# Batched 64x64 matrix products: two output rows to a partition, and all DMAs on one queue

## The chip, the cores and the metric

One core of a Trainium2 chip. The metric is the device time in microseconds of one execution, slowest core (there is only one). Engines are named as in the profile: PE (TensorE), PEld (its weight loads), DVE (VectorE), ACT (ScalarE), POOL (GpSimd), SP (SyncE). DMAs are issued from an engine's queue and carried by 16 DMA engines. DMAs issued from POOL use what the profile calls queue 0, "software_dynamic"; those issued from SP use queue 1, "hardware_dynamic".

## The reference

```python
# a, b: [1024, 64, 64] float32, normally distributed
def reference(a, b):
    return np.matmul(a, b).astype(np.float32)
```

16.8 MB of each input are read and 16.8 MB are written. A row of a matrix is 64 floats, 256 contiguous bytes.

## The kernel before

The batch is worked in 16 groups of 64 matrices. Loads are issued from POOL and cast fp32 to bf16 on the way. PE transposes `a`, multiplies, DVE and ACT copy the products out of PSUM, and SP issues the stores.

```python
    a_v = a.rearrange("(g u hc) r n -> g hc r u n", u=U_LG, hc=4)
    b_v = b.rearrange("(g s h) r n -> g h r s n", s=S_LG, h=2)
    o_v = out.rearrange("(g s h) r n -> g h r s n", s=S_LG, h=2)
    ...
    for lg in range(n_lg):
        a_ld = lg_pool.tile([128, U_LG, 128], bf16, name="a_ld")
        b_ld = lg_pool.tile([128, S_LG, 64], bf16, name="b_ld")
        # loads: nc.gpsimd.dma_start(...), 4 for a and 2 for b, runs of 256 bytes in DRAM
        ...
        o_sb = lg_pool.tile([128, S_LG, 64], fp32, name="o_sb")
        for cg in range(n_cg):
            # 8 transposes of 128x128, one copy to at_sb, 32 products of 64x64, copies to o_sb
            ...
        for s0 in range(0, S_LG, S_CG):
            nc.sync.dma_start(
                out=o_v[lg, :, :, s0 : s0 + S_CG, :],
                in_=o_sb[:, s0 : s0 + S_CG, :],
            )
```

In `o_v` a partition is one row of a matrix, so each contiguous piece of a store is one row: 256 bytes.

Of the kernel before, what the change touches and what calls it, by code (L numbers as in the profile page):

```python
# [1 line left out]

# [5 lines left out]

fp32 = mybir.dt.float32  # L10
bf16 = mybir.dt.bfloat16


@with_exitstack
def kernel(
    ctx: ExitStack,
    tc: tile.TileContext,
    a: bass.AP,
    b: bass.AP,
    out: bass.AP,  # L20
):
    nc = tc.nc

    B, M, K = a.shape
    _, _, N = b.shape
    assert (M, K, N) == (64, 64, 64)

    LG = 64 if B % 64 == 0 else 32
    CG = 32
    CAST_ON_DMA = True  # L30
    SBUF_BUFS = 3
    PSUM_BUFS = 2

    assert B % LG == 0 and LG % CG == 0
    n_lg = B // LG
    n_cg = LG // CG

    U_LG = LG // 4
    S_LG = LG // 2
    U_CG = CG // 4  # L40
    S_CG = CG // 2
    BANK_SLOTS = 8

    a_v = a.rearrange("(g u hc) r n -> g hc r u n", u=U_LG, hc=4)
    b_v = b.rearrange("(g s h) r n -> g h r s n", s=S_LG, h=2)
    o_v = out.rearrange("(g s h) r n -> g h r s n", s=S_LG, h=2)

    consts = ctx.enter_context(tc.tile_pool(name="consts", bufs=1))
    lg_pool = ctx.enter_context(tc.tile_pool(name="lg", bufs=SBUF_BUFS))
    cg_pool = ctx.enter_context(tc.tile_pool(name="cg", bufs=2 * PSUM_BUFS))  # L50
    ps_pool = ctx.enter_context(
        tc.tile_pool(name="ps", bufs=PSUM_BUFS, space=bass.MemoryType.PSUM)
    )

    identity = consts.tile([128, 128], bf16)
    make_identity(nc, identity)

    for lg in range(n_lg):
        ld_dt = bf16 if CAST_ON_DMA else fp32
        a_ld = lg_pool.tile([128, U_LG, 128], ld_dt, name="a_ld")  # L60
        b_ld = lg_pool.tile([128, S_LG, 64], ld_dt, name="b_ld")

        for h in range(2):
            for c in range(2):
                nc.gpsimd.dma_start(  # L65
                    out=a_ld[64 * h : 64 * h + 64, :, 64 * c : 64 * c + 64],
                    in_=a_v[lg, 2 * h + c],
                )
        for s0 in range(0, S_LG, S_CG):
            nc.gpsimd.dma_start(  # L70
                out=b_ld[:, s0 : s0 + S_CG, :],
                in_=b_v[lg, :, :, s0 : s0 + S_CG, :],
            )

        if CAST_ON_DMA:
            a_sb, b_sb = a_ld, b_ld
        else:
            a_sb = lg_pool.tile([128, U_LG, 128], bf16, name="a_sb")
            b_sb = lg_pool.tile([128, S_LG, 64], bf16, name="b_sb")
            nc.vector.tensor_copy(a_sb[:], a_ld[:])  # L80
            nc.scalar.copy(b_sb[:], b_ld[:])

        o_sb = lg_pool.tile([128, S_LG, 64], fp32, name="o_sb")

        for cg in range(n_cg):
            u0 = cg * U_CG
            s_base = cg * S_CG

            at_ps = ps_pool.tile([128, U_CG, 128], bf16, name="at_ps")
            for uu in range(U_CG):  # L90
                nc.tensor.transpose(  # L91
                    at_ps[:, uu, :], a_sb[:, u0 + uu, :], identity
                )
            at_sb = cg_pool.tile([128, U_CG, 128], bf16, name="at_sb")
            nc.vector.tensor_copy(at_sb[:], at_ps[:])  # L95

            o_ps = ps_pool.tile([128, S_CG, 64], fp32, name="o_ps")
            for sl in range(S_CG):
                s = s_base + sl
                for h in range(2):  # L100
                    rows = slice(64 * h, 64 * h + 64)
                    nc.tensor.matmul(  # L102
                        o_ps[rows, sl, :],
                        at_sb[rows, sl // 2, 64 * (sl % 2) : 64 * (sl % 2) + 64],
                        b_sb[rows, s, :],
                        start=True,
                        stop=True,
                    )

            for k in range(0, S_CG, BANK_SLOTS):  # L110
                src = o_ps[:, k : k + BANK_SLOTS, :]
                dst = o_sb[:, s_base + k : s_base + k + BANK_SLOTS, :]
                if (cg + k // BANK_SLOTS) % 2 == 0:
                    nc.vector.tensor_copy(dst, src)  # L114
                else:
                    nc.scalar.copy(dst, src)  # L116

        for s0 in range(0, S_LG, S_CG):
            nc.sync.dma_start(
                out=o_v[lg, :, :, s0 : s0 + S_CG, :],  # L120
                in_=o_sb[:, s0 : s0 + S_CG, :],
            )


# [1 line left out]
_INS = ['a', 'b']  # L126
_OUTS = [((1024, 64, 64), 'float32')]


# [23 lines left out]
```

## Time and profile before

| | before |
|---|---|
| median of 5 runs | 222.24 us (221.48 to 223.13) |
| span in the profile | 220.5 us |
| busy: PE, DVE, ACT | 29%, 20%, 9% |
| DMA packets: loads, stores | 131,072, 65,536 |

These are lines from the page of the kernel before. The first gives busy time and share of the span by engine. `DMA` and `GB/s` are 40 slices of the span: tenths of the DMA engines' time, and what they moved. The `q` lines give packets, MB and the packets' summed time as a share of 16 engines' span (packets overlap, so it can pass 100%). Then come the chain of waits by engine ("issue" is time in which an engine waited for nothing that the profile shows), and the DMA issues with the size of one and its time to landing.

```profile
span 220.5 us, 3019 instructions
PE 63.7 (29%) x1280; PEld 56.7 (26%) x1280; DVE 44.3 (20%) x64; ACT 20.0 (9%) x33; POOL 89.8 (41%) x102
...
DMA  7999999999999999999999999999999999999974
GB/s 49 139 155 158 159 158 158 158 158 156 158 158 159 158 156 161 157 158 158 157 158 158 158 157 158 158 160 158 157 157 159 155 158 157 158 159 156 169 149 95
...
q0 software_dynamic: 132608, 16.78, 117.7%
q1 hardware_dynamic: 66048, 16.78, 55.7%
...
DMA 81%; POOL 13%; issue 3%; PE 0%; DVE 0%; ACT 0%; POOLq 0%
...
out_dram<-o_sb SPq DMA_DIRECT2D x32, 512.0 KB, 11.0
a_ld<-in_a_dram POOLq DMA_DIRECT2D x64, 128.0 KB, 15.2
b_ld<-in_b_dram POOLq DMA_DIRECT2D x32, 256.0 KB, 20.0
```

DMA stands at 9 from the second slice to nearly the end, it is 81% of the chain, and no compute engine is above 30%. GB/s is a flat 158. A 9 alone does not show that the engines never idle: the digit adds up the packets' times, which overlap (by the q lines, 173% of the span here), and stops at 9. The q lines also count packets of 4 bytes; without them there are 131,072 loads and 65,536 stores.

To see what a packet costs, I counted the trace's packet records in stretches of 4 us and fitted (least squares, leaving out the start and the end) how much of one DMA engine's time each kind takes. Three stretches of the kernel before, and the fit:

```
stretch from the first packet, us   loads   stores   ns of one engine per packet
128 to 132                           4779        0   13.4
152 to 156                           1642     1653   19.4
164 to 168                           1614     1629   19.7
fit: 13.3 ns per load, 25.7 ns per store
sum: 131,072 x 13.3 / 16 = 109 us;  65,536 x 25.7 / 16 = 105 us
```

The two prices together give back the 16 engines' time in every stretch closely (scatter 0.6%), so the engines were busy throughout. "Fit" below always means this.

### The profile page before, as it was taken

To read this page: it belongs to the slowest core of one execution; us is meant where nothing else is said; L and a number is where in the kernel's file an instruction comes from. 1 tells how busy PE (TensorE), PEld (TensorE's weight loads), DVE (VectorE), ACT (ScalarE), POOL (GpSimd) and SP (SyncE) were. 2 spreads that over 40 slices of the span, in tenths; PEclk is the share of its full clock that TensorE was granted. 3 is DMA by queue.
4 is the path that set the end of the run, shared out by engine and by line. 5 is a ranking of instruction groups with operands and counts; after the bars stand their busy time and mean duration, and the time that the engine had idled before them with its cause. 6 is when DMAs were issued, how large, how long until landed. Compare 5 with 4: busy or idle time off the path is not lost.

```text
span 220.5 us, 3019 instructions
## 1 busy us (share of the span) xinstructions
PE 63.7 (29%) x1280; PEld 56.7 (26%) x1280; DVE 44.3 (20%) x64; ACT 20.0 (9%) x33; POOL 89.8 (41%) x102
## 2 busy tenths in 40 slices
PE   0443131142321425123341133403323241222420
PEld 0433121142320414122231133303322231222310
DVE  0223121122211312103131031312113131031211
ACT  2021101102011020200211002110110202001020
POOL 8994441625425354161632427334262542600000
DMA  7999999999999999999999999999999999999974
GB/s 49 139 155 158 159 158 158 158 158 156 158 158 159 158 156 161 157 158 158 157 158 158 158 157 158 158 160 158 157 157 159 155 158 157 158 159 156 169 149 95
DMA packets 198669, 33.74 MB, mean 153 GB/s; under 512 B 198657, under 2 KB 198657, under 8 KB 198657
## 3 DMA queue, kind: packets, MB, share of 16 engines
q0 software_dynamic: 132608, 16.78, 117.7%
q1 hardware_dynamic: 66048, 16.78, 55.7%
q8 instruction: 10, 0.16, 0.3%
q14 instruction: 3, 0.02, 0.0%
HBM read 33.55 MB, written 16.78 MB: 228 GB/s over the span
## 4 chain that ended last, share of the span: by engine, by line
DMA 81%; POOL 13%; issue 3%; PE 0%; DVE 0%; ACT 0%; POOLq 0%
DMA b_ld<-in_b_dram 60%; DMA a_ld<-in_a_dram 21%; POOL a_ld L65 8%; POOL b_ld L70 5%; PE o_ps L102 0%; DVE o_sb L114 0%; ACT o_sb L116 0%; POOL identity masks.py:199 0%; POOL identity masks.py:197 0%; POOLq masks.py:199 0%; POOLq L70 0%; POOLq L148 0%; POOLq L137 0%
## 5 line engine op out<-in xcount | busy, mean ns | idle before, releaser
L65 POOL DMA_DIRECT2D a_ld<-in_a_dram x64 | 52.6, 833 | 86.8 <-DMA b_ld<-in_b_dram 74.9
L102 PE MATMUL o_ps<-b_ld,at_sb 64*64 64x64 bf16 x1024 | 34.0, 238 | 79.0 <-DMA b_ld<-in_b_dram 79.0
L102 PEld LDWEIGHTS <-at_sb 64*64 64x64 bf16 x1024 | 30.6, 151 | 84.3 <-issue 79.1
L91 PE MATMUL at_ps<-identity,a_ld 128*128 128x128 bf16 x256 | 29.8, 309 | 71.6 <-DMA a_ld<-in_a_dram 71.6
L91 PEld LDWEIGHTS <-a_ld 128*128 128x128 bf16 x256 | 26.0, 143 | 73.1 <-issue 68.2
L70 POOL DMA_DIRECT2D b_ld<-in_b_dram x32 | 37.1, 1169 | 15.9 <-DMA a_ld<-in_a_dram 14.3
L114 DVE COPY o_sb<-o_ps 128x512 f32<-128x512 f32 x32 | 22.1, 692 | 100.6 <-ACT o_sb L116 60.7
L116 ACT COPY o_sb<-o_ps 128x512 f32<-128x512 f32 x32 | 18.8, 586 | 194.1 <-DVE o_sb L114 153.8
L95 DVE COPY at_sb<-at_ps 128x1024 bf16<-128x1024 bf16 x32 | 22.1, 692 | 70.8 <-PE at_ps L91 70.8
L116 ACT ACT_TABLE_LOAD x1 | 1.3, 1283 | 0.7 <-PEq L137 0.7
masks.py:199 POOL TENSOR_SCALAR_AFFINE_SELECT identity<-identity 128x128 bf16<-128x128 bf16 x1 | 0.3, 306 | 0.1
masks.py:197 POOL MEMSET identity<- 128x128 bf16 x1 | 0.2, 205 | 0.3 <-POOLq L137 0.3
L137 POOL MEMSET const-float32-0.0<- 128x1 f32 x1 | 0.1, 99 | 0.2 <-issue 0.2
L137 POOL MEMSET const-bfloat16-1.0<- 128x1 bf16 x1 | 0.1, 102 | 0.0
L137 POOL MEMSET const-uint8-127<- 128x1 uint8 x1 | 0.1, 102 | 0.0
L137 POOL MEMSET const-float32-1.0<- 128x1 f32 x1 | 0.1, 99 | 0.0
## 6 DMA issues: line engine op xcount, KB each, us to landing
out_dram<-o_sb SPq DMA_DIRECT2D x32, 512.0 KB, 11.0
a_ld<-in_a_dram POOLq DMA_DIRECT2D x64, 128.0 KB, 15.2
b_ld<-in_b_dram POOLq DMA_DIRECT2D x32, 256.0 KB, 20.0
```

The source lines that it names most:

```text
L65: nc.gpsimd.dma_start(out=a_ld[64 * h : 64 * h + 64, :, 64 * c : 64 * c + 64], in_=a_v[lg, 2 * h + c],)
L70: nc.gpsimd.dma_start(out=b_ld[:, s0 : s0 + S_CG, :], in_=b_v[lg, :, :, s0 : s0 + S_CG, :],)
L91: nc.tensor.transpose(at_ps[:, uu, :], a_sb[:, u0 + uu, :], identity)
L95: nc.vector.tensor_copy(at_sb[:], at_ps[:])
L102: nc.tensor.matmul(o_ps[rows, sl, :], at_sb[rows, sl // 2, 64 * (sl % 2) : 64 * (sl % 2) + 64], b_sb[rows, s, :], start=True, stop=True,)
L114: nc.vector.tensor_copy(dst, src)
L116: nc.scalar.copy(dst, src)
L137: nc = _bacc.Bacc("TRN2", target_bir_lowering=False, num_devices=1)
```

## The change

Three things at once. Stores get runs of 512 contiguous bytes: a partition holds two neighbouring output rows. The stores move from SP's queue to POOL's, behind the loads. The order on POOL is fixed by hand, with loads two groups ahead of the compute. To produce row pairs, `a` is loaded block-diagonally (two matrices on the diagonal of a 128x128 block, zeros kept from one memset), which doubles the transposes, and the products take every second row of `a` as their weights. Smaller things change with it: compute groups of 16 matrices instead of 32, three PSUM buffers instead of two, one store of 1 MB per group (two for the last group) instead of two of 512 KB. The diff's core:

```diff
-    o_v = out.rearrange("(g s h) r n -> g h r s n", s=S_LG, h=2)
+    a_tiles = []
+    for ai in range(A_BUFS):                       # A_BUFS = 3
+        a_diag = a_pool.tile([128, P2_LG, 128], bf16, name=f"a_diag_{ai}")
+        nc.vector.memset(a_diag, 0.0)
+        a_tiles.append(a_diag)
+    def load_a(lg):
+        a_sb = a_tiles[lg % A_BUFS]
+        for h in range(2):
+            nc.gpsimd.dma_start(
+                out=a_sb[64 * h : 64 * h + 64, :, 64 * h : 64 * h + 64],
+                in_=a_v[lg, h],
+            )
     ...
+        o_dst = out[i0 : i0 + LG].rearrange(
+            "(q b4) (t u) c -> b4 t q u c", b4=4, u=2
+        )
     ...
+                for j in range(2):
                     nc.tensor.matmul(
-                        o_ps[rows, sl, :],
-                        at_sb[rows, sl // 2, 64 * (sl % 2) : 64 * (sl % 2) + 64],
-                        b_sb[rows, s, :],
+                        o_ps[orows, sigma, 64 * j : 64 * j + 64],
+                        stat[:, :, j::2],
+                        b_sb[:, p, :],
     ...
-            nc.sync.dma_start(
-                out=o_v[lg, :, :, s0 : s0 + S_CG, :],
-                in_=o_sb[:, s0 : s0 + S_CG, :],
-            )
+                nc.gpsimd.dma_start(out=o_dst[:, :, q0:q1], in_=o_sb[:, q0:q1, :])
+    with tc.manual_schedule(engines={mybir.EngineType.Pool}):
+        load_b(0); load_a(0); load_a(1); load_b(1)      # four lines in the kernel
+        for lg in range(n_lg):
+            if lg + 2 < n_lg:
+                load_a(lg + 2)
+                load_b(lg + 2)
+            compute_and_store(lg)
```

More of the change, by code (lines that the diff above doesn't have):

```diff
@@ L26 @@
     assert (M, K, N) == (64, 64, 64)
-    LG = 64 if B % 64 == 0 else 32
-    CG = 32
-    CAST_ON_DMA = True
+    LG = 64 if B % 64 == 0 else B
+    CG = 16
+    STORE_BF16 = False
+    A_BUFS = 3
     SBUF_BUFS = 3
-    PSUM_BUFS = 2
+    PSUM_BUFS = 3
     assert B % LG == 0 and LG % CG == 0
@@ L36 @@
     n_cg = LG // CG
-    U_LG = LG // 4
-    S_LG = LG // 2
-    U_CG = CG // 4
-    S_CG = CG // 2
-    BANK_SLOTS = 8
-    a_v = a.rearrange("(g u hc) r n -> g hc r u n", u=U_LG, hc=4)
-    b_v = b.rearrange("(g s h) r n -> g h r s n", s=S_LG, h=2)
-    o_v = out.rearrange("(g s h) r n -> g h r s n", s=S_LG, h=2)
+    P2_LG = LG // 2
+    P2_CG = CG // 2
+    S4_CG = CG // 4
+    a_v = a.rearrange("(g p h) r n -> g h r p n", p=P2_LG, h=2)
+    b_v = b.rearrange("(g s h) r n -> g h r s n", s=P2_LG, h=2)
     consts = ctx.enter_context(tc.tile_pool(name="consts", bufs=1))
+    a_pool = ctx.enter_context(tc.tile_pool(name="a_pool", bufs=1))
     lg_pool = ctx.enter_context(tc.tile_pool(name="lg", bufs=SBUF_BUFS))
@@ L56 @@
     make_identity(nc, identity)
-    for lg in range(n_lg):
-        ld_dt = bf16 if CAST_ON_DMA else fp32
-        a_ld = lg_pool.tile([128, U_LG, 128], ld_dt, name="a_ld")
-        b_ld = lg_pool.tile([128, S_LG, 64], ld_dt, name="b_ld")
-        for h in range(2):
-            for c in range(2):
-                nc.gpsimd.dma_start(
-                    out=a_ld[64 * h : 64 * h + 64, :, 64 * c : 64 * c + 64],
-                    in_=a_v[lg, 2 * h + c],
-                )
-        for s0 in range(0, S_LG, S_CG):
-            nc.gpsimd.dma_start(
-                out=b_ld[:, s0 : s0 + S_CG, :],
-                in_=b_v[lg, :, :, s0 : s0 + S_CG, :],
-            )
-        if CAST_ON_DMA:
-            a_sb, b_sb = a_ld, b_ld
-        else:
-            a_sb = lg_pool.tile([128, U_LG, 128], bf16, name="a_sb")
-            b_sb = lg_pool.tile([128, S_LG, 64], bf16, name="b_sb")
-            nc.vector.tensor_copy(a_sb[:], a_ld[:])
-            nc.scalar.copy(b_sb[:], b_ld[:])
-        o_sb = lg_pool.tile([128, S_LG, 64], fp32, name="o_sb")
-        for cg in range(n_cg):
-            u0 = cg * U_CG
-            s_base = cg * S_CG
-            at_ps = ps_pool.tile([128, U_CG, 128], bf16, name="at_ps")
-            for uu in range(U_CG):
-                nc.tensor.transpose(
-                    at_ps[:, uu, :], a_sb[:, u0 + uu, :], identity
-                )
-            at_sb = cg_pool.tile([128, U_CG, 128], bf16, name="at_sb")
-            nc.vector.tensor_copy(at_sb[:], at_ps[:])
-            o_ps = ps_pool.tile([128, S_CG, 64], fp32, name="o_ps")
-            for sl in range(S_CG):
-                s = s_base + sl
-                for h in range(2):
-                    rows = slice(64 * h, 64 * h + 64)
@@ new lines, with load_b @@
+    a_tiles = []
[3 more added lines that the diff above has]
+        a_tiles.append(a_diag)
+    out_dt = bf16 if STORE_BF16 else fp32
+    b_tiles = {}
+    def load_a(lg):
+        a_sb = a_tiles[lg % A_BUFS]
+        for h in range(2):
+            nc.gpsimd.dma_start(
+                out=a_sb[64 * h : 64 * h + 64, :, 64 * h : 64 * h + 64],
+                in_=a_v[lg, h],
+            )
+    def load_b(lg):
+        b_sb = lg_pool.tile([128, P2_LG, 64], bf16, name="b_sb")
+        for s0 in range(0, P2_LG, P2_LG // 2):
+            nc.gpsimd.dma_start(
+                out=b_sb[:, s0 : s0 + P2_LG // 2, :],
+                in_=b_v[lg, :, :, s0 : s0 + P2_LG // 2, :],
+            )
+        b_tiles[lg] = b_sb
@@ new lines, in compute_and_store @@
+    def compute_and_store(lg):
+        i0 = lg * LG
+        a_sb = a_tiles[lg % A_BUFS]
+        b_sb = b_tiles.pop(lg)
+        o_sb = lg_pool.tile([128, LG // 4, 128], out_dt, name="o_sb")
+        o_dst = out[i0 : i0 + LG].rearrange(
+            "(q b4) (t u) c -> b4 t q u c", b4=4, u=2
+        )
+        for cg in range(n_cg):
+            p0 = cg * P2_CG
+            t_ps = ps_pool.tile([128, P2_CG, 128], bf16, name="t_ps")
+            for pp in range(P2_CG):
+                nc.tensor.transpose(
+                    t_ps[:, pp, :], a_sb[:, p0 + pp, :], identity
+                )
+            t_sb = cg_pool.tile([128, P2_CG, 128], bf16, name="t_sb")
+            nc.vector.tensor_copy(t_sb[:], t_ps[:])
+            o_ps = ps_pool.tile([128, S4_CG, 128], fp32, name="o_ps")
+            for pp in range(P2_CG):
+                p = p0 + pp
+                sigma, colp = pp // 2, pp % 2
+                orows = slice(64 * colp, 64 * colp + 64)
+                stat = t_sb[:, pp, :].rearrange("k (hh mm) -> k hh mm", hh=2)
+                for j in range(2):
@@ L108 @@
                     )
-            for k in range(0, S_CG, BANK_SLOTS):
-                src = o_ps[:, k : k + BANK_SLOTS, :]
-                dst = o_sb[:, s_base + k : s_base + k + BANK_SLOTS, :]
-                if (cg + k // BANK_SLOTS) % 2 == 0:
-                    nc.vector.tensor_copy(dst, src)
-                else:
-                    nc.scalar.copy(dst, src)
-        for s0 in range(0, S_LG, S_CG):
-            nc.sync.dma_start(
-                out=o_v[lg, :, :, s0 : s0 + S_CG, :],
-                in_=o_sb[:, s0 : s0 + S_CG, :],
-            )
+            half = S4_CG // 2
+            dst = o_sb[:, cg * S4_CG : (cg + 1) * S4_CG, :]
+            nc.vector.tensor_copy(dst[:, :half, :], o_ps[:, :half, :])
+            nc.scalar.copy(dst[:, half:, :], o_ps[:, half:, :])
+            pieces = 2 if lg == n_lg - 1 else 1
+            if (cg + 1) % (n_cg // pieces) == 0:
+                q1 = (cg + 1) * S4_CG
+                q0 = q1 - (n_cg // pieces) * S4_CG
+                nc.gpsimd.dma_start(out=o_dst[:, :, q0:q1], in_=o_sb[:, q0:q1, :])
+    with tc.manual_schedule(engines={mybir.EngineType.Pool}):
+        load_b(0)
+        load_a(0)
+        load_a(1)
+        load_b(1)
+        for lg in range(n_lg):
[3 more added lines that the diff above has]
+            compute_and_store(lg)
 _INS = ['a', 'b']
```

## The prediction

> **What bounds the kernel now.** DMA. The page's slices show DMA at 9 tenths in nearly every slice and 155 to 160 GB/s, the chain of waits is 81% DMA (60% b loads, 21% a loads), while PE is busy 29%, DVE 20%, ACT 9%. The DMA section counts 131,072 load packets (queue 0; 256 bytes read, 128 written as bf16) and 65,536 store packets of 256 bytes (queue 1).
>
> I counted the trace's packet records in stretches of 4 us. Where only loads run, one engine of the 16 takes 13.3 ns per packet; where loads and stores alternate one to one, 19.4 ns. A least-squares fit gives 13.3 ns per load and 25.7 ns per store. The sum: 131,072 x 13.3 / 16 = 109 us, and 65,536 x 25.7 / 16 = 105 us, together 214 of the 220.5 us span. The other 6.7 us are the start (first packet near 3 us), the fill and the end. So half the time is the stores, at twice the price of a load with the same 256 bytes at the HBM end.
>
> **What the change does.** It pairs two output rows in one partition, so a store moves 512 contiguous bytes: 32,768 store packets instead of 65,536. Loads keep their packets (131,072 of 256 bytes). To get there it doubles the transposes (512 of 128x128, half of each zeros) and keeps 1,024 products of 64 output columns, now over 128 rows.
>
> The price of a 512-byte store is the one disputed term. The Trainium skill's page "DMA: Bandwidth & Descriptors" says in "Specifications" that under 512 bytes the DMA does a read-modify-write, which fits the 25.7 against 13.3 ns here; and in "Why small descriptors are slow" it counts bytes/32 + 3 cycles, 11 for 256 bytes, which at the page's 850 MHz is 12.9 ns against the measured 13.3. By the same rule an estimate for 512 bytes is 19 cycles, 22.4 ns. Stores: 32,768 x 22.4 / 16 = 46 us instead of 105.
>
> **Off the critical path**, per group of 64 matrices, against a DMA period of 6.8 + 2.9 = 9.7 us (estimates from the timeline's durations): PE 32 transposes at 0.116 us plus 64 products at 0.033 us = 5.8 us; DVE 4 x 0.69 + 4 x about 0.4 = 4.4 us; POOL five issues at about 1.2 us = 6 us. All fit, PE and POOL at about 60%. The stores move to POOL's queue, in order behind the loads, and a store waits for its group's compute; but loads for two more groups are issued ahead of it, about 10 us of queued packets, so the queue should not run dry. The three memsets run while POOL issues b, and cost at most about 1 us. At the end, the last group's compute (about 7 us) runs under the stores of the two groups before it, and its store is split in two.
>
> **Predicted.** Packets 109 + 46 = 155 us; edges 6.7 plus about 2 for the last store: span 164 us; the measured time is 1.7 us over the span: 166 us, range 159 to 182. Faster by over 2%: 0.95; within 2%: 0.03; slower: 0.02.
>
> **What would show it.** Right: 32,768 packets of 512 bytes, about 22 ns each in the fit, loads still 13.3 ns; DMA still 9 tenths throughout; steady rate near 210 GB/s; chain still DMA. Wrong: stores at 38 ns or more (a cost that grows with bytes: 196 us; at 51 ns no gain at all); DMA slices with holes while POOL waits for ACT's or DVE's copies (the in-order queue runs dry); POOL issues much longer than 1.2 us while DVE copies; PE above 9 us per group.

## More of the kernel before

The loop over `lg` is ordered by a scheduler; beyond the three buffers of each tile (`SBUF_BUFS = 3`), nothing in the kernel fixes how far the loads run ahead.

A price from the fit is a spacing, how much later the next packet is done. It is not how long one packet is in flight, which is longer when packets overlap.

## The result

| | before | changed |
|---|---|---|
| median | 222.64 us (15 runs) | 159.84 us (8 runs, 159.37 to 160.45) |
| ratio, 95% interval | | 0.7187 (0.7172 to 0.7201) |
| span in the profile | 220.5 us | 157.9 us |

Ratios are the mean time of one kernel's fast runs over that of the other's of the same rounds, so not quite the ratio of the medians.

The page of the changed kernel, the same lines:

```profile
span 157.9 us, 3573 instructions
PE 86.9 (55%) x1536; PEld 72.8 (46%) x1536; DVE 73.5 (47%) x131; ACT 25.1 (16%) x65; POOL 91.5 (58%) x87
...
PEclk9999996958576595678959577595857659567585
DMA  2999999999999999999999999999999999999984
GB/s 15 147 155 156 156 161 318 154 293 183 201 271 158 314 160 256 220 172 301 158 298 176 215 259 159 317 155 271 204 184 290 158 304 169 238 237 170 366 306 132
DMA packets 136480, 33.79 MB, mean 214 GB/s; under 512 B 132368, under 2 KB 132368, under 8 KB 136464
...
q0 software_dynamic: 136464, 33.56, 195.2%
...
DMA 46%; issue 19%; POOL 18%; PE 13%; POOLq 1%
...
L99 PE MATMUL t_ps<-identity,a_diag 128*128 128x128 bf16 x512 | 55.9, 286 | 58.1 <-DMA a_diag<-in_a_dram 58.1
L103 DVE COPY t_sb<-t_ps 128x1024 bf16<-128x1024 bf16 x64 | 43.3, 690 | 66.3 <-PE t_ps L99 66.0
...
L122 DVE COPY o_sb<-o_ps 128x256 f32<-128x256 f32 x64 | 27.0, 423 | 9.7 <-PE o_ps L112 9.7
...
out_dram<-o_sb POOLq DMA_DIRECT2D x15, 1024.0 KB, 13.5
b_sb<-in_b_dram POOLq DMA_DIRECT2D x32, 256.0 KB, 12.4
a_diag<-in_a_dram POOLq DMA_DIRECT2D x32, 256.0 KB, 12.6
```

DMA is still at 9 in every slice up to the end, the fit (scatter 2%) again leaves no idle stretch, and DMA is still the largest part of the chain. What changed is what it moves in that time: GB/s swings between about 155 and 315, low where only loads run and high where stores run. Both kernels move the same bytes. Queue 1 is gone.

The line of DMA packets holds a surprise. The prediction announced 32,768 store packets of 512 bytes, but the packets between 2 KB and 8 KB number 136,464 - 132,368 = 4,096. The packet records show them: each store packet has 4,096 bytes, eight runs of 512. So the software queue gathered the stores into larger packets. Its loads, which cast, stay at one run per packet. The fit gives 13.2 ns per load and 166 ns per store packet, which is 20.7 ns per 512 bytes. The sum is 108.1 + 4,096 x 166 / 16 = 42.5, together 150.6 us; the rest of the span, 7.3 us, is the edges.

So two things came at once for the stores: longer runs, and another queue that gathers. The prediction had credited the first alone. The experiments take them apart.

### The profile page after: what moved, and what is told of

The parts are those of the page before. It is cut to its first block, busy times and chain, and to the rows that moved or that the text cites. A ratio compares the mean times of both kernels' runs of the same rounds, so it can differ in the third digit from the quotient of the medians.

```text
span 157.9 us, 3573 instructions
## 1 busy us (share of the span) xinstructions
PE 86.9 (55%) x1536; PEld 72.8 (46%) x1536; DVE 73.5 (47%) x131; ACT 25.1 (16%) x65; POOL 91.5 (58%) x87
## 2 busy tenths in 40 slices
DMA packets 136480, 33.79 MB, mean 214 GB/s; under 512 B 132368, under 2 KB 132368, under 8 KB 136464
## 3 DMA queue, kind: packets, MB, share of 16 engines
q0 software_dynamic: 136464, 33.56, 195.2%
## 4 chain that ended last, share of the span: by engine, by line
DMA 46%; issue 19%; POOL 18%; PE 13%; POOLq 1%
DMA a_diag<-in_a_dram 46%; POOL a_diag L70 9%; PE t_ps L99 8%; POOL b_sb L78 5%; PE o_ps L112 4%; POOL out_dram L130 3%; POOLq L168 1%; POOL identity masks.py:199 0%; POOL identity masks.py:197 0%; POOLq masks.py:199 0%; POOLq L78 0%; POOLq L130 0%; POOLq L70 0%; POOLq L157 0%
## 5 line engine op out<-in xcount | busy, mean ns | idle before, releaser
L99 PE MATMUL t_ps<-identity,a_diag 128*128 128x128 bf16 x512 | 55.9, 286 | 58.1 <-DMA a_diag<-in_a_dram 58.1
L103 DVE COPY t_sb<-t_ps 128x1024 bf16<-128x1024 bf16 x64 | 43.3, 690 | 66.3 <-PE t_ps L99 66.0
L99 PEld LDWEIGHTS <-a_diag 128*128 128x128 bf16 x512 | 44.9, 130 | 61.2 <-issue 52.5
L70 POOL DMA_DIRECT2D a_diag<-in_a_dram x32 | 34.8, 1095 | 27.4 <-DMA out_dram<-o_sb 21.2
L78 POOL DMA_DIRECT2D b_sb<-in_b_dram x32 | 37.1, 1166 | 13.5 <-DMA a_diag<-in_a_dram 7.0
L123 ACT COPY o_sb<-o_ps 128x256 f32<-128x256 f32 x64 | 23.8, 372 | 126.1 <-DVE o_sb L122 126.1
L112 PE MATMUL o_ps<-b_sb,t_sb 128*64 128x64 bf16 x1024 | 35.7, 224 | 6.1 <-DVE t_sb L103 5.2
L112 PEld LDWEIGHTS <-t_sb 128*64 128x64 bf16 x1024 | 27.9, 135 | 16.9 <-DVE t_sb L103 16.5
L122 DVE COPY o_sb<-o_ps 128x256 f32<-128x256 f32 x64 | 27.0, 423 | 9.7 <-PE o_ps L112 9.7
L130 POOL DMA_DIRECT2D out_dram<-o_sb x17 | 19.2, 1132 | 20.3 <-ACT o_sb L123 15.0
```

The costliest lines, as they stand in the source:

```text
L70: nc.gpsimd.dma_start(out=a_sb[64 * h : 64 * h + 64, :, 64 * h : 64 * h + 64], in_=a_v[lg, h],)
L78: nc.gpsimd.dma_start(out=b_sb[:, s0 : s0 + P2_LG // 2, :], in_=b_v[lg, :, :, s0 : s0 + P2_LG // 2, :],)
L99: nc.tensor.transpose(t_ps[:, pp, :], a_sb[:, p0 + pp, :], identity)
L103: nc.vector.tensor_copy(t_sb[:], t_ps[:])
L112: nc.tensor.matmul(o_ps[orows, sigma, 64 * j : 64 * j + 64], stat[:, :, j::2], b_sb[:, p, :], start=True, stop=True,)
L122: nc.vector.tensor_copy(dst[:, :half, :], o_ps[:, :half, :])
```

## The experiments

Each edit is against the changed kernel unless it says otherwise. The theory of the prediction is S: a store under 512 bytes pays double, whatever the queue. The first rival is Q: the gain is POOL's queue with its gathering. From e5 on, P is the law for packets that e5's expectation states, and Q the queue as such. e5 to e8 ran on another chip than e1 to e4 and e9 to e12; the kernel before took 222.51 us there and 222.57 to 222.79 here.

### e1: only the queue, in the kernel before

```diff
-            nc.sync.dma_start(          # the store
+            nc.gpsimd.dma_start(
```

> The kernel before with one change: its 256-byte stores are issued from POOL's queue, not SP's. Theory S (size: a 256-byte store costs 25.7 ns because it is under 512 bytes): about 222 us, stores still near 25 ns per 256 bytes in the fit. Theory Q (queue: the changed kernel's trace records its stores as packets of 4,096 bytes, so the software queue gathers store descriptors into large packets, and that is the gain): stores recorded as 4,096-byte packets, about 11 ns per 256 bytes, 109 + 45 us, so about 162 us, up to 180 if the stores' waits in POOL's queue let the DMA run dry.

Measured: 245.38 us, ratio 1.1019 (1.1003 to 1.1036): slower by 10%. Neither theory's time. The stores were gathered (4,096 packets of 4,096 bytes, sixteen runs of 256), a median of 304 ns in flight, which is 19 ns per 256 bytes. That is less than the 25.7 ns of SP's queue, so the price is not what lost the time. POOL's queue now stood still for the stores. The waits of e1 (engine, line, what it waited for, us in total, times, longest):

```profile
PE at_ps L91 <- DMA a_ld<-in_a_dram: 152.9, 16, 11.4
...
POOL out_dram L119 <- ACT o_sb L116: 98.2, 16, 8.2
```

POOL waited 98 us for copies that its next stores need, and the loads behind those stores waited with it. The median time from issue to landing of an `a` load fell from 15.2 us to 7.9 us, which suggests that far fewer packets were queued. The packet records show the holes: leaving out 12 us at each end, there are 16 us in e1 in which no packet at all was in flight, and none in the kernel before or the changed one. (The digits of e1's DMA row hide this: in those slices they stay at 7 to 9.) The changed kernel has the same in-order queue, and its POOL waited only 15.0 us for ACT; its hand-made order issues two groups of loads before it reaches a store. e3 below has e1's kind of packets in that order and takes 184.54 us, 61 us less. The two also differ in the computation and in the size of an issue, so that the order alone makes the difference is likely, not shown.

### e2, e3, e4: run length and queue, one at a time

```diff
 e2   -  nc.gpsimd.dma_start(out=o_dst[:, :, q0:q1], in_=o_sb[:, q0:q1, :])
      +  nc.sync.dma_start(out=o_dst[:, :, q0:q1], in_=o_sb[:, q0:q1, :])

 e3   -  o_sb = lg_pool.tile([128, LG // 4, 128], ...)       # the two rows of a pair adjacent
      +  o_sb = lg_pool.tile([128, LG // 2, 64], ...)        # viewed as [128, u, q, 64]
      -      "(q b4) (t u) c -> b4 t q u c"
      +      "(q b4) (t u) c -> (b4 t) u q c"                # runs of 256 bytes, one DMA as before

 e4   e3's layout, with nc.sync.dma_start
```

> The changed kernel with one change: its 512-byte stores go out from SP's queue again. Theory S: the size alone matters, stores about 21 ns per 512 bytes whatever the queue, time within 2% of 160 us. Theory Q: without the gathering, each store is a packet of 512 bytes; if the cost is one per packet near 25.7 ns, 32,768 x 25.7 / 16 = 53 us and about 170 us in all; if it goes by bytes (51 ns), about 222 us.

> The changed kernel with its stores still on POOL's queue, in as many issues, but cut into runs of 256 bytes (the two rows of a pair lie apart in the partition). Theory S: stores back to about 25 ns per 256 bytes, 105 us, total near 220 us. Theory Q: stores gathered into 4,096-byte packets, 11 to 13 ns per 256 bytes, total 160 to 172 us.

> The changed kernel's computing with the kernel before's way of storing: runs of 256 bytes from SP's queue. Both theories: stores 25.7 ns per 256 bytes and a time within 2% of 222 us, which says that the doubled transposes, the block-diagonal form and the deeper loads neither cost nor gain anything beside the stores. If it is under 215 us, part of the gain comes from the order of the loads.

Measured:

| | SP's queue | POOL's queue |
|---|---|---|
| runs of 256 bytes | e4: 217.18 us in its one fast run | e3: 184.54 us (0.8282, 0.8264 to 0.8300) |
| runs of 512 bytes | e2: 189.67 us (0.8522, 0.8505 to 0.8540) | changed kernel: 159.84 us |

The other three runs of e4, 220.75 to 222.57 us, lie more than 1.5% above that one. Its profile (a slow run) gives fits of 13.2 and 25.8 ns, like the kernel before. So the new computation with the old way of storing takes about the old time: the doubled transposes cost nothing that shows, and what is not the stores' is at most 2 to 3% of the old time (5 of the 63 us gained).

Neither S nor Q is right alone. From the kernel before, the length by itself (e2) brings 33 us and the queue then 30 us more; taken the other way, the queue by itself (e3) brings 38 us and the length then 25 us. The fits account for the first path: stores on SP's queue cost 25.7 ns per 256 bytes, then 35.3 ns per 512 (32,768 x 35.3 / 16 = 72 us, 33 less than 105), then 20.7 ns per 512 on POOL's queue (42.5 us, 30 less).

e3 needs care, for its chain is no longer DMA's:

```profile
POOL 46%; issue 39%; DMA 6%; PE 2%; POOLq 1%; DVE 1%; ACT 0%
...
POOL out_dram L136 <- ACT o_sb L130: 57.6, 14, 4.9
```

POOL waited 57.6 us for ACT's copies before its stores, so the DMA engines may have run dry. DMA stays at 9 tenths from the second slice on, which settles nothing, and e3's fit is loose (scatter 10%). But its store packets are longer in flight (mean 260 ns against 172 in the changed kernel). Gathered packets run about one at a time (172 ns in flight for a price of 166), so their flights can be added up: with 13.2 ns per load, this estimate leaves the engines idle for about 3 us of e3 between the ends, and for less than 1 us of the changed kernel. So most of e3's 25 us are dearer packets.

The DMA queues of e2:

```profile
q0 software_dynamic: 132096, 16.78, 139.2%
q1 hardware_dynamic: 33040, 16.78, 42.5%
```

A store of e2 is a packet of its own, 32,768 of them, in flight 40 ns (median). The share fell from 55.7% of a 220.5 us span to 42.5% of 187.9 us, so from 123 to 80 us: half the packets, each longer.

### e5: 2,048-byte runs on SP's queue (wrong result)

```diff
-            "(q b4) (t u) c -> b4 t q u c", b4=4, u=2
+            "(q pa) (pb w) c -> (pa pb) q (w c)", q=4, w=8    # lands in wrong places
-                nc.gpsimd.dma_start(...)
+                nc.sync.dma_start(out=o_dst[:, q0 // 4 : q1 // 4, :], in_=...)
```

> Wrong result on purpose: the stores go out from SP's queue in contiguous runs of 2,048 bytes (4 times as long), to wrong places. Theory P (every packet of a store costs one engine a fixed 16 ns plus its bytes at 26.7 GB/s, worked out from the fits of 25.7 ns for 256 and 35.3 ns for 512 bytes; the software queue gains because it puts 4,096 bytes in a packet): 8,192 packets at about 93 ns, 48 us, total about 163 to 168 us. Theory Q (it is POOL's queue as such): stores stay near 35 ns per 512 bytes, total 189 us.

Measured: 164.54 to 165.47 us in its three fast runs (0.7416, 0.7393 to 0.7440). The fit of its profile, which was a slow run 1.5% above the fastest, is 92.7 ns per packet against the 93 expected. So theory P's law for SP's queue holds over a factor of eight in length: **beside POOL's loads, a store packet costs a DMA engine about 16 ns, plus its bytes at 26.7 GB/s** (25.7, 35.3 and 92.7 ns for 256, 512 and 2,048 bytes). There is no step at 512 bytes in it.

### e6: 256-byte pieces side by side in DRAM (wrong result)

```diff
+        o_sb = lg_pool.tile([128, LG // 4, 2, 72], ...)     # gaps in SBUF keep pieces of 256 bytes
+            "pa (pb w) c -> (pa pb) w c", w=32              # one partition's pieces adjacent in DRAM
```

> Wrong result on purpose: stores on POOL's queue in pieces of 256 bytes, as in the run with 256-byte pieces before it, but the pieces of one partition lie side by side in DRAM. In that earlier run, gathered packets took 195 ns in one mode and about 300 ns in another. If the 300 ns mode comes from where the pieces land in DRAM, nearly all packets now take 195 ns or less and the total is 162 to 170 us. If it comes from the 256-byte pieces themselves, it stays near 184 us with the two modes.

Measured: 181.20 us (0.8144, 0.8106 to 0.8181), with both modes still there: median 195 ns, mean 246 (e3: 195 and 260). Where the pieces land matters little; the price comes with the 256-byte pieces. The slow mode shows plainly in the end part of e3, where stores run alone: 4 us held 191 packets, 16 x 4,000 / 191 = 335 ns of an engine each.

### e7, e8: loads without the cast

If gathering helped stores, it might help loads. They would then have to be plain copies, with the cast done by ACT (e7: `b` only) or by ACT and DVE (e8: both).

```diff
-        b_sb = lg_pool.tile([128, P2_LG, 64], bf16, name="b_sb")
+        b_ld = lg_pool.tile([128, P2_LG, 64], fp32, name="b_ld")
     ...
+            nc.scalar.copy(b_sb[:, p0 : p0 + P2_CG, :], b_ld[:, p0 : p0 + P2_CG, :])
```

> Correct result. b is loaded as fp32, without the cast in the DMA, and cast by ACT. If loads without a cast are gathered into 4,096-byte packets as the stores are, b packets number 4,096 and cost about 160 to 170 ns, 10 to 10.6 ns per 256 bytes instead of 13.2: about 11 to 13 us less, total about 148 us. If gathering has nothing to do with the cast, b stays in packets of its own and the total stays at 160 us.

> Correct result. Both a and b are loaded as fp32 and cast by ACT and DVE. With gathering for both: loads 131,072 x 10 to 10.6 ns / 16 = 82 to 87 us, stores 43 us, edges about 8 us: 133 to 140 us; up to 150 if DVE (about 6.6 us of a 7.9 us period) and ACT delay the stores. Without gathering: 160 us or more.

Measured: e7 168.83 and 169.40 us (its two fast runs), e8 193.33 us (0.8680, 0.8661 to 0.8698, against the kernel before). Both are slower than the changed kernel, and far from the expected 148 and 133 to 140 us. The loads were gathered as expected, and they were dearer. DMA packets and rate of e8:

```profile
GB/s 87 218 219 218 215 218 267 290 217 337 224 277 283 224 345 216 307 268 247 331 228 344 231 298 288 254 337 248 320 276 278 327 255 350 254 332 280 327 196 147
DMA packets 13601, 50.57 MB, mean 264 GB/s; under 512 B 1296, under 2 KB 1296, under 8 KB 13584
```

In its first slices only loads run, at a flat 218 GB/s. In the packet records, 4 us hold 210 packets of 4,096 bytes there: 305 ns each, 19.0 ns per 256-byte run, against 13.2 ns for a cast load in a packet of its own. (Two things differ at once: the gathered loads do not cast, and write 256 bytes to SBUF where the cast loads write 128. Single loads without a cast were not run.) That is the slow mode of e3 and e6 again, now for loads. So a gathered packet of sixteen 256-byte runs costs about 300 ns where such packets run alone, while one of eight 512-byte runs takes 174 ns. Gathering is not the gain in itself.

### e9: 512-byte runs for the loads of a (wrong result)

```diff
-    a_v = a.rearrange("(g p h) r n -> g h r p n", p=P2_LG, h=2)
+    a_v = a.rearrange("(g q pa) (pb w) n -> g (pa pb) q (w n)", q=P2_LG // 2, pa=4, w=2)
-                out=a_sb[64 * h : 64 * h + 64, :, 64 * h : 64 * h + 64],
+                out=a_sb[64 * h : 64 * h + 64, : P2_LG // 2, :],
```

> Wrong result on purpose: a is loaded, still with the cast, in runs of 512 bytes instead of 256 (half as many packets), into the wrong order. If a cast load's price is mostly per packet (packets of loads overlap, so a longer one costs little more), 32,768 of them at 14 to 16 ns: 24 us less, about 136 us. If it goes by the page's count (19 cycles, 22.4 ns, an estimate): 54 us becomes 46 us, about 151 us. If by bytes: no change, 160 us.

Measured: 153.57 us (0.6893, 0.6878 to 0.6908). The fit gives 23.7 ns per 512-byte cast load (22.5 if a stretch counts the packets that end in it, so it is good to about 1 ns). This is the middle of the three expectations, the count of the Trainium skill's page "DMA: Bandwidth & Descriptors", section "Why small descriptors are slow" (an estimate of 22.4 ns). For cast loads that count agrees at both lengths: 13.2 ns measured against 12.9, and 23.7 against 22.4.

### e10: 2,048-byte runs on POOL's queue (wrong result)

The edit is e5's, with the store left on `nc.gpsimd`.

> Wrong result on purpose: stores on POOL's queue in runs of 2,048 bytes, two descriptors to a packet of 4,096 instead of eight. The packets should take about 155 to 162 ns instead of 174 (the shortest taken by 512-byte ones were 161), 2 to 4 us in all: 156 to 158 us. It tells how much of the gap between 256 and 512 bytes inside a gathered packet is a threshold: from 512 to 2,048 the step should be small.

Measured: 157.05 us (0.7046, 0.7031 to 0.7061); the fit is 157 ns per packet. Inside a gathered packet, 512 bytes cost 30 ns at 256-byte runs (e3), 20.7 at 512 and 19.6 at 2,048. Here there is a step between 256 and 512, and nearly nothing after it.

### e11: a store that casts, on POOL's queue

```diff
-    STORE_BF16 = False
+    STORE_BF16 = True         # o_sb is bf16, the DMA casts to fp32 on the way out
```

> The result is rounded to bf16 and so less exact: o_sb is bf16 and the DMA casts it to fp32 on its way out, from the same queue, in the same issues, in the same 512-byte runs at DRAM. The records of the cast loads suggest that a cast is never gathered. Theory P (packets of 4,096 bytes are the gain): stores become 32,768 packets of their own, at about 35 ns as from SP's queue, total about 185 to 190 us. If they overlap like cast loads, down to 22 ns, 160 us. Theory Q (POOL's queue is the gain): 160 us with single packets. If the cast stores are gathered after all, the run says nothing.

Measured: 162.36 us (0.7285, 0.7271 to 0.7299), correct. DMA packets and queue of e11:

```profile
DMA packets 165152, 33.79 MB, mean 211 GB/s; under 512 B 132368, under 2 KB 165136, under 8 KB 165136
...
q0 software_dynamic: 165136, 33.56, 248.9%
```

This run shows that gathering is not needed for the low price, against theory P. The stores were not gathered: 165,136 - 132,368 = 32,768 packets between 512 bytes and 2 KB, as in e2. Yet they cost 21.9 ns each, not 35.3. They were in flight longer than in e2 (median 64 ns against 40), and the queue's share passes 240%: 64 / 21.9 = 2.9 packets at a time, where e2's stores have 40 / 35.3 = 1.1. So these stores overlap, as cast loads do (32 / 13.2 = 2.4), and on SP's queue they hardly do. Two differences beside the queue remain: e11's stores cast, and they read half the bytes from SBUF. Every kind of packet that clearly overlaps in this case casts, and no run has single stores without a cast on POOL's queue. Whether the overlap belongs to the queue or to the cast is therefore not shown.

The store's price in all runs, from the fits:

```
          run at DRAM   queue   recorded as            ns per packet   ns per 512 bytes   median in flight, ns
before     256 bytes    SP      256 bytes                   25.7             51.4                31
e2         512          SP      512                         35.3             35.3                40
e5       2,048          SP      2,048                       92.7             23.2                96
e3         256          POOL    4,096 (gathered)           240               30.0               195
e6         256          POOL    4,096 (gathered)           234               29.3               195
changed    512          POOL    4,096 (gathered)           166               20.7               174
e10      2,048          POOL    4,096 (gathered)           157               19.6               159
e11        512, cast    POOL    512                         21.9             21.9                64
```

These are prices beside loads. After the last load, each trace ends with stores that run alone, and their packet records give another price (e5's trace is of its slow run):

```
          queue   store packets, in the densest stretch   ns per packet   in flight at a time   median in flight, ns
before     SP     1,728 of 256 bytes in 2 us                   18.5             0.97                  18
e2         SP     858 of 512 in 1.5 us                         28.0             1.03                  29
e5         SP     191 of 2,048 in 1 us                         83.8             1.02                  86
changed    POOL   192 of 4,096 in 2 us                        167               1.02                 174
e11        POOL   1,448 of 512, cast, in 2 us                  22.1             2.96                  67
```

Alone, too, SP's stores run one at a time, so it is not the loads that keep them from overlapping. But each is 7 to 9 ns cheaper than beside POOL's loads, at all three lengths, while the two kinds of POOL's stores listed here cost the same alone as beside them. So of the 14.6 ns by which a 512-byte store is dearer on SP's queue than on POOL's (35.3 against 20.7), about half is there only while the other queue's loads run: an estimate of 32,768 x 7.3 / 16 = 15 of the queue's 30 us.

### e12: a version that beats both

What e9 pointed to, made correct. `a` is loaded two rows to a partition, in 512-byte runs. PE, which has room, undoes the pairing: 1,024 small products of `a` with half of the identity's columns bring each matrix's `a`-transpose to the half of the partitions where its `b` lies. DVE and ACT copy the halves into block-diagonal tiles whose zeros were set once. The main products are as before.

```diff
+    a_v = a.rearrange("(g q b4) (t u) n -> g (b4 t) q (u n)", q=LG // 4, b4=4, u=2)
+    idh = identity[:].rearrange("p (b h t) -> p h b t", b=2, h=2)
+                for u, h in ((0, 0), (0, 1), (1, 0), (1, 1)):
+                    nc.tensor.matmul(t_ps[64 * h : 64 * h + 64, qq, u],
+                                     a_sb[:, q, 64 * u : 64 * u + 64], idh[:, h], ...)
+            nc.vector.tensor_copy(t_sb[:64, :, :, :, 0], t_ps[:64])
+            nc.scalar.copy(t_sb[64:, :, :, :, 1], t_ps[64:])
```

> Correct result: a version meant to beat both kernels. a is loaded in runs of 512 bytes, two rows to a partition, and the pairing is undone by 1,024 small products with the identity's columns, whose result is put block-diagonally into t_sb; everything after that is as in the changed kernel. From the fit of the run with 512-byte loads into the wrong order: b 65,536 x 12.7 / 16 = 52 us, a 32,768 x 23.7 / 16 = 49 us, stores 4,096 x 171 / 16 = 44 us, edges 7 to 8 us and 1.6 us over the span: 152 to 156 us against the changed kernel's 160. If DVE's and ACT's larger copies from PSUM (estimates of 4.5 and 3.8 us per group against a DMA period of 9.1 us) delay the stores, 156 to 162 us.

Measured: correct, 154.09 us (153.49 to 154.84; ratio 0.6918, 0.6887 to 0.6948, against the kernel before). That is 5.75 us or 3.6% under the changed kernel's median, from runs of different rounds but the same kernel before (222.79 and 222.64 us). (It also has four PSUM buffers instead of three.) Lines of its page:

```profile
span 152.4 us, 4708 instructions
PE 66.8 (44%) x2048; PEld 59.7 (39%) x2048; DVE 70.6 (46%) x136; ACT 62.0 (41%) x129; POOL 84.7 (56%) x87
...
PEclk9999969555555555555555555555555555555555
DMA  1999999999999999999999999999999999999992
```

DMA is at 9 again, the fit has a scatter of 1%, and the chain is 64% DMA and 2% ACT, so the added copies on ACT (62 us busy against 25) cost little. The TensorE clock granted was 0.58 of full speed, against 0.74 in the changed kernel's profile, and this is the fastest of all correct runs: PE does not bound it. The same is seen in the kernel before, whose runs had clocks from 0.53 to 1.00 at 221.8 to 223.5 us.

## Why the prediction was right, and where it was not

- **What bounds.** Right. The prices of the fit fill the engines' time in the stretches before and after, and the sum of packets explains the span with 6.7 us left before and 7.3 us after.
- **The loads.** Right: 131,072 packets at 13.2 ns, 108 us (predicted 109).
- **Off the critical path.** Right. PE took 86.9 / 16 = 5.4 us per group (predicted 5.8), DVE's copies (43.3 + 27.0) / 16 = 4.4 (4.4), POOL 91.5 / 16 = 5.7 (6). The queue did not run dry, and POOL's waits for ACT came to 15.0 us. e4 shows the computation costs nothing that can be seen beside the old stores, e1 how POOL's queue can run dry.
- **The price of a store.** The number was close (22.4 ns; 20.7 measured) and its reason was incomplete. The step that failed is "under 512 bytes the DMA does a read-modify-write, which fits the 25.7 against 13.3 ns here", and from it 22.4 ns for a 512-byte store on any queue. e2 makes exactly that store on SP's queue: 35.3 ns and 189.67 us, far outside the predicted range. With length alone the gain is 33 us, not 59. The other 30 us came with the queue, which the prediction treated only as a question of order ("behind the loads"). No packet of the changed kernel is the 512-byte store that was counted; that 22.4 lay near the 20.7 of a gathered run is luck.
- **What it announced of the profile.** The count of 32,768 packets of 512 bytes was wrong: they are 4,096 packets of 4,096 bytes. The steady rate near 210 GB/s was about right (226 from 20 to 140 us, 214 over the whole span).
- **The 6 us by which it was too high.** Stores 46 predicted, 42.5 measured (3.4 us); loads 0.9 us; edges 8.7 predicted, 7.3 measured (1.4 us); time over the span 0.2 us more than assumed. That makes 5.5 us; the rest is rounding, for the unrounded sum of the prediction was 165.3.

What stays open: why stores of SP's queue do not overlap. The ends of the traces exclude the loads of the other queue as the cause; the kind of queue and the missing cast remain. (The gathered packets of POOL's queue, which do not cast, run one at a time too: 1.02 in the last table.) Why sharing the engines with POOL's loads adds 7 to 9 ns to each of SP's stores is open too. In the stretches where both ran, the two kinds came one to one (1,642 loads to 1,653 stores), which fits the queues taking turns, but no run tests it. Also open is what makes a gathered packet of 256-byte runs take 195 ns in one mode and 300 in another; e6 excludes where in DRAM the pieces lie side by side as the main cause, and e8 shows that it is not special to stores.

## What to carry to other kernels

When DMA is full and rows are short, price a packet of each kind from the trace, and price the queue with the length: here lengthening the run and changing the queue were worth 33 and 30 us (25 and 38 in the other order), and only one of them was in the prediction. Take the price where the kinds run together as well as alone: a 512-byte store of SP's queue cost 35.3 ns beside the other queue's loads and 28.0 alone. And do not read a 9 in the DMA row as proof of full engines where packets overlap. Before moving stores to the queue that issues the loads, fix the order so that loads are issued well ahead, or the stores' waits can hold the loads up (e1: 10% slower, with 16 us in which nothing was in flight). And do not take gathering into large packets as a gain in itself: it left stores of 512 bytes about where single overlapping packets had them (20.7 and 21.9 ns), and the gathered loads of 256 bytes, which no longer cast, were dearer than single ones that did (19.0 against 13.2 ns).

## What the Trainium skill lacked or had wrong

- "DMA: Bandwidth & Descriptors", section "Rules for kernel authors": it says that spreading DMAs over issuing engines does not help bandwidth and saves only issue time, and it sends simple stores to Sync in "Issuing engine by pattern". Here the queue changed the price of the same 512-byte store from 35.3 ns (SP's, beside loads from POOL's) to 20.7 (POOL's), and the time from 189.67 to 159.84 us. No page has a price for stores of one queue beside loads of another: 35.3 ns against 28.0 alone.
- The same page, "Specifications" (512 bytes as the least transfer for line rate, read-modify-write below): on SP's queue, beside loads, stores cost 16 ns plus bytes at 26.7 GB/s from 256 to 2,048 bytes, with no step at 512. A step shows only in gathered packets on POOL's queue: 30.0, 20.7 and 19.6 ns per 512 bytes for runs of 256, 512 and 2,048.
- The same page, "SWDGE vs HWDGE vs iDMA", gives a packet as preferably up to 4,096 bytes. Plain copies on POOL's queue agree (two runs of 2,048, eight of 512 or sixteen of 256 in 4,096 bytes). It lacks that a DMA with a cast is not gathered: 131,072 loads, and e11's 32,768 stores, were packets of their own.
- The same page, "Why small descriptors are slow": its count of bytes/32 + 3 cycles fits cast loads (13.2 ns measured for 12.9, 23.7 for 22.4). It says that putting descriptors together is only worth it at 256 bytes or less; that it pays there is not borne out by the loads here, for gathered fp32 loads of 256 bytes cost 19.0 ns each and single cast loads 13.2, but the cast differs too, and no run has both forms of one transfer.
